# Softmax scaling of the larger half moved to ScalarE, and five weight units of the attention's queries multiplied as plain fp32

## The chip, the cores and the metric

The kernel runs on one core of one Trainium2 chip. The metric is the device time of one execution in microseconds (us). TensorE multiplies (PE in the profile, with PEld for its weight loads), VectorE is DVE, ScalarE is ACT, GpSimd is POOL, and SyncE (SP) issues the loads of the weights.

## The reference, cut to what matters

The reference is a stack of blocks on 256 tokens of width 1024 in fp32: feed-forward blocks, a recurrent block, one dilated attention, and two hybrid mixer layers. The change lies in the dilated attention alone:

```python
q = (x @ w_q).reshape(bsz, s, N_GROUPS, N_HEADS, HEAD_DIM)     # 3 groups, 16 heads of 64
scores = einsum("bpnqhd,bpnkhd->bpnhqk", qb, kw) / sqrt(dh)
scores = where(valid, scores - slope * distance, NEG_INF)
p = exp(scores - max(scores)); denom = sum(p)
out = einsum("bpnhqk,bpnkhd->bpnqhd", p / denom, vw)            # per group
out = sum over groups of softmax(log-sum-exp) * out             # then @ w_o
```

With one shared maximum per query, the sum over the three groups and the division by one common denominator give the same result as the softmax over the groups.

## The kernel before

All weights stream through one list of 537 units. A unit is 128 x 1024 fp32 (512 KB): eight 128 x 128 weight tiles in the order in which they are multiplied. SP loads each unit into one of five raw buffers (`RAWS = 5`, line 96). Then the unit is split for three fast multiplications: ACT rounds it to fp32r in two casts of 128 x 512 (`whi`, line 108), and DVE subtracts to get the remainder, again in two instructions of 128 x 512 (`wlo`, line 122). The raw buffer is free after the second subtraction. `whi` and `wlo` have seven buffers each, and `pump` prepares units up to `LOOK = 6` ahead of the one in use. The activations are held in two parts as well (`gh`, `gl`), so one weight tile costs three multiplications in `mm3` (line 174 through `mm`).

Units in the set `NATIVE` take another way: no cast and no subtraction, and one plain fp32 multiplication of the raw tile with the unsplit activations (`xf`, or `uc` and `xg`). Their raw buffer is free only when the last multiplication of the unit has read it. Before the change these are units 74 and 77 to 90 (the recurrent block: its gates and its GELU branch) and 347 to 352.

```python
def _hi(self):                          # lines 99 to 109
    ...
    if u in NATIVE:
        return
    ...
def mm3(self, out, w, xh, xl, start, stop, x=None):   # lines 176 to 182
    if w[1] is None:
        self.mm(out, w[0], x, start, stop)
        return
    self.mm(out, w[0], xh, start, False)
    self.mm(out, w[0], xl, False, False)
    self.mm(out, w[1], xh, False, stop)
```

The attention (`attn`, line 687) uses units 249 to 280. Units 249 to 252 are the first four query tiles, multiplied while the layer norm before is finished (`filler`). Units 253 and 254 hold the two tiles of the third group for head pairs 0 and 1, with the k index outside; 254 is k = 4 to 7. After that every two units make one call of `group`: for A = 2, 4, 6 units (A, groups 0 and 1), (A and A+1, group 2), (A+1, groups 0 and 1), so that 257 is (A=2, group 2), 260 the second tile of pair 3, 263 (A=4, group 2), and 266 the second tile of pair 5. Units 267 to 272 are pairs 6 and 7, and 273 to 280 the output projection.

Between the groups, `step` works a pipeline over heads (order in `PLAN`): `scores(h)` (12 multiplications on PE, bias and minimum on DVE line 744, exponential on ACT line 747), `soft(h-1)`, `trans(h-2)` (three transposes on PE, line 185, and a copy on ACT, line 768) and `pv(h-3)` (four multiplications). `put` (lines 724 and 725) splits the queries on ACT and DVE. POOL loads keys and values of the pairs (`K`, `W`, lines 700 and 701) and does the first addition of `soft`.

Dependences and the order on each engine come from the tile framework: it orders the instructions of each engine ahead of the run, by priority and by its own estimate of times, and inserts the waits. Each engine then runs its list in that order, so an instruction that waits holds up all behind it on its engine.

Of the kernel before, what the change touches and what calls it, by code (L numbers as in the profile page):

```python
# [12 lines left out]
AF = mybir.ActivationFunctionType  # L13
ALU = mybir.AluOpType
# [24 lines left out]
HOOKS = (1, 3, 5)  # L39
KVB = 5  # L40
RAWS = 5
NATIVE = {*range(347, 353), 74, 77, 78, 81, 84, 79, 80, 82, 83, *range(85, 91)}
RAW_LN = (LN_EMB - 1,)
LATE = {347: (6, 5)}

# [31 lines left out]
class Builder:  # L77
# [21 lines left out]
    def _hi(self):  # L99
# [3 lines left out]
        self.nhi += 1  # L103
        if u in NATIVE:
            return
# [5 lines left out]
    def _lo(self, pool=False):  # L111
# [3 lines left out]
        self.nlo += 1  # L115
        if u in NATIVE:
            return
# [16 lines left out]
    def w(self, spec, n=1):  # L134
# [3 lines left out]
        if o == 0:  # L138
            self.his.pop(u - 1, None)
            self.los.pop(u - 1, None)  # L140
            if u - 1 in NATIVE:
                self.raws.pop(u - 1)
# [7 lines left out]
        else:  # L150
            self.plan.extend(spec)
        if u in NATIVE:
            return self.raws[u][:, o * 128:(o + n) * 128], None
# [533 lines left out]
    def attn(self, ln_in, ln_out, eps):  # L687
        nc = self.nc
        N, off = SEQ, META
        with self.tc.tile_pool(name="attn", bufs=1) as p:  # L690
# [59 lines left out]
            def soft(h):  # L750
                s, den = S.pop(h), DEN.pop(h)
                nc.vector.reciprocal(den, den)
                t = p.tile([128, 384], F32, tag="t", name="t", bufs=4)
                for i, (a, n) in enumerate(((0, 256), (768, 128))):
                    o = t[:, 0:256] if i == 0 else t[:, 256:384]
                    nc.gpsimd.tensor_tensor(o, s[:, a:a + n], s[:, a + n:a + 2 * n], op=ALU.add)
                    nc.vector.tensor_tensor(o, o, s[:, a + 2 * n:a + 3 * n], op=ALU.add)  # L757
                    nc.vector.tensor_scalar(o, o, den[:, i:i + 1], None, op0=ALU.mult)
                S[h] = t

            def trans(h):
# [25 lines left out]
            def step(n=1):  # L787

                for _ in range(n):
                    i = next(steps)  # L790
                    if i < N_HEADS:
                        scores(i)
                    if 0 <= i - 1 < N_HEADS:
                        soft(i - 1)
                    if 0 <= i - 2 < N_HEADS:
                        trans(i - 2)
                    if 0 <= i - 3 < N_HEADS:
                        pv(i - 3)
# [714 lines left out]
```

## Time and profile before

| | |
|---|---|
| median of 3 runs | 1732.87 us (1731.61 to 1736.07) |
| profiled execution | 1732.95 us, span 1731.2 us |
| mean granted TensorE clock | 0.991 |
| PE busy | 1684.8 us (97%) |
| DVE busy | 1212.1 us (70%) |
| ACT busy | 1011.6 us (58%) |
| POOL busy | 166.0 us (10%) |

The span runs from the first to the last instruction of the profiled execution; 1.75 us of its time lie around it. Shares are averages over the whole span; the attention is some 7% of it. The granted clock is given as a share of 2.4 GHz: 1.00 is 2.4 GHz, 0.50 is 1.2 GHz. A plain fp32 multiplication of 128 x 256 leaves two records of TensorE in the trace, an fp32r one leaves one. Matmul records overlap, so the time that one takes is read from a stretch (busy time over count), not from its own duration.

### The profile page before, as it was taken

The page shows a single profiled execution, that of the slowest core. Times are in us where ns is not written, and L with a number is a line of the kernel's source. Part 1 is how long each engine was busy: PE and PEld are TensorE (multiplying, and loading weights), DVE is VectorE, ACT ScalarE, POOL GpSimd, SP SyncE. Part 2 cuts the span into 40 slices and gives each one's busy share as a digit, 9 for nine tenths or more (in the row PEclk, how much of TensorE's full clock was granted, in tenths as well). Part 3 has the DMA queues.
Part 4 walks back from the last instruction along what each step waited for, and adds up shares of the span by engine and source line. Part 5 has one row for each costly group of instructions (what it writes and reads, how often), then busy time and mean ns, then how long its engine had stood idle before and what let it go on. Part 6 is the DMA issues. An engine that isn't in the chain of part 4 may idle for free.

```text
span 1731.2 us, 34185 instructions
## 1 busy us (share of the span) xinstructions
PE 1684.8 (97%) x13420; PEld 1644.2 (95%) x13420; DVE 1212.1 (70%) x2377; ACT 1011.6 (58%) x2061; POOL 166.0 (10%) x240
## 2 busy tenths in 40 slices
PE   8999999999999999988999999899999999999996
PEld 8999999999999999988899999789999998999996
DVE  7666788965675666698897655878955577696653
ACT  6544756744575545576675455766744467585443
POOL 0001100000110000332110002121000122010011
PEclk9999999999999999989999999999999999999998
DMA  8555436555548655574236555243555545346550
GB/s 299 189 186 184 135 131 226 194 192 185 182 150 300 205 184 184 183 218 149 90 122 229 188 187 191 98 139 106 183 178 176 176 168 164 99 144 218 187 184 25
DMA packets 85594, 300.05 MB, mean 173 GB/s; under 512 B 11372, under 2 KB 13688, under 8 KB 85176
## 3 DMA queue, kind: packets, MB, share of 16 engines
q1 hardware_dynamic: 80216, 283.79, 49.2%
q0 software_dynamic: 2736, 9.61, 2.0%
q10 hardware_dynamic: 2480, 4.46, 0.8%
q8 instruction: 105, 1.72, 0.4%
q14 instruction: 57, 0.47, 0.1%
HBM read 292.47 MB, written 5.24 MB: 172 GB/s over the span
## 4 chain that ended last, share of the span: by engine, by line
PE 86%; DVE 7%; ACT 4%; issue 2%; DMA 1%; POOL 0%; DVEq 0%; SPq 0%; ACTq 0%
PE ps L174 86%; DVE wlo L122 2%; ACT whi L108 1%; PE ps L185 1%; DMA raw<-in_wst_dram 1%; DVE gl L258 1%; DVE q L725 1%; DVE s L744 1%; DVE xf L296 0%; DVE acc L235 0%; ACT q L724 0%; DVE xf L355 0%; DVE xf L354 0%; ACT fv L364 0%; DVE t L757 0%
## 5 line engine op out<-in xcount | busy, mean ns | idle before, releaser
L122 DVE TENSOR_TENSOR wlo<-raw,whi 128x512 fp32r<-128x512 f32 x1032 | 681.6, 697 | 332.6 <-ACT whi L108 331.5
L108 ACT CAST whi<-raw 128x512 fp32r<-128x512 f32 x1032 | 592.0, 617 | 493.4 <-issue 307.1
L174 PE MATMUL ps<-gh,whi 128*128 128x256 f32 (+3 forms) x2736 | 782.4, 287 | 7.4 <-ACT whi L108 6.7
L174 PE MATMUL ps<-gl,whi 128*128 128x256 f32 (+3 forms) x2736 | 777.6, 284 | 0.9 <-DVE gl L344 0.8
L174 PE MATMUL ps<-gh,wlo 128*128 128x256 f32 (+3 forms) x2736 | 774.4, 283 | 0.0
L174 PEld LDWEIGHTS ps<-gh,whi 128*128 128x128 f32 x2736 | 517.3, 189 | 11.5 <-ACT whi L108 7.9
L174 PEld LDWEIGHTS ps<-gl,whi 128*128 128x128 f32 x2736 | 518.8, 190 | 3.4 <-DVE gl L344 1.5
L174 PEld LDWEIGHTS ps<-gh,wlo 128*128 128x128 f32 x2736 | 519.4, 190 | 0.3 <-issue 0.2
L174 PE MATMUL ps<-hh,wlo 128*128 128x256 f32 (+1 forms) x1056 | 298.0, 282 | 0.0
L174 PE MATMUL ps<-hh,whi 128*128 128x256 f32 (+1 forms) x1056 | 297.9, 282 | 0.0
L174 PE MATMUL ps<-hl,whi 128*128 128x256 f32 (+1 forms) x1056 | 297.7, 282 | 0.0
L174 PEld LDWEIGHTS ps<-hl,whi 128*128 128x128 f32 x1056 | 199.0, 188 | 0.0
L174 PEld LDWEIGHTS ps<-hh,whi 128*128 128x128 f32 x1056 | 199.0, 188 | 0.0
L174 PEld LDWEIGHTS ps<-hh,wlo 128*128 128x128 f32 x1056 | 198.8, 188 | 0.0
L234 POOL TENSOR_TENSOR acc<-xf 128x256 f32<-128x256 f32 (+1 forms) x10 | 7.6, 756 | 1087.2 <-DVE xf L296 1085.0
L494 DVE TENSOR_TENSOR th<-th,ps 128x512 f32<-128x512 f32 (+1 forms) x62 | 42.9, 692 | 52.3 <-PE ps L174 52.2
L234 POOL TENSOR_TENSOR acc<-acc,xf 128x256 f32<-128x256 f32 (+1 forms) x50 | 46.9, 939 | 204.0 <-DVE xf L296 189.8
L296 DVE SCALAR_TENSOR_TENSOR xf<-ps,xf 128x256 f32<-128x256 f32 (+1 forms) x80 | 32.9, 423 | 43.0 <-PE ps L174 42.9
L239 ACT ACTIVATE sq<-xf 128x256 f32<-128x256 f32 (+1 forms) x88 | 35.6, 410 | 41.2 <-DVE xf L296 32.4
L252 ACT ACTIVATE gh<-xf,prm 128x256 fp32r<-128x256 f32 (+1 forms) x64 | 32.2, 509 | 46.4 <-DVE xf L296 46.4
L258 DVE SCALAR_TENSOR_TENSOR gl<-xf,prm,gh 128x256 fp32r<-128x256 f32 (+1 forms) x64 | 40.4, 638 | 11.0 <-ACT gh L252 11.0
L338 ACT ACTIVATE xf<-nt,prm 128x256 f32<-128x256 f32 (+1 forms) x72 | 42.6, 604 | 6.8 <-DVE nt L336 6.6
(319 smaller groups left out, 1842.0 us busy)
## 6 DMA issues: line engine op xcount, KB each, us to landing
raw<-in_wst_dram SPq DMA_DIRECT2D x537, 512.0 KB, 3.6
K<-khl POOLq DMA_DIRECT2D x32, 128.0 KB, 6.2
cst<-in_c_mix_dram POOLq DMA_DIRECT2D x2, 1202.0 KB, 5.8
khl<-kh ACTq DMA_DIRECT2D x4, 512.0 KB, 6.8
vsc<-kt ACTq DMA_DIRECT2D x4, 512.0 KB, 6.8
W<-vsc POOLq DMA_DIRECT2D x8, 256.0 KB, 5.8
out_dram<-xf SPq DMA_DIRECT2D x8, 128.0 KB, 1.7
dt<-in_c_dist_dram POOLq DMA_DIRECT2D x1, 576.0 KB, 9.6
```

The lines of the kernel that those rows point to most:

```text
L108: self.nc.scalar.copy(hi[:, q:q + 512], self.raws[u][:, q:q + 512])
L122: eng.tensor_tensor(lo[:, q:q + 512], r[:, q:q + 512], h[:, q:q + 512], op=ALU.subtract)
L174: self.nc.tensor.matmul(out, lhsT, rhs, start=start, stop=stop, skip_group_check=True)
L185: self.nc.tensor.matmul(out, in_, self.ident[0:n, 0:n], start=True, stop=True, is_transpose=True, skip_group_check=True)
L234: eng.tensor_tensor(a[:, 0, 0:N], x0, x, op=ALU.add)
L239: self.nc.scalar.activation(sq[:, 0:N], self.xf[:, m, off:off + N], AF.Square)
L252: return self.nc.scalar.activation((self.xg if ln in RAW_LN else self.gh)[:, m, c], self.xf[:, m, off:off + N], AF.Copy, scale=g)
L258: return self.nc.vector.scalar_tensor_tensor(self.gl[:, m, c], self.xf[:, m, off:off + N], g, self.gh[:, m, c].bitcast(F32), op0=ALU.mult, ...
L296: self.nc.vector.scalar_tensor_tensor(x, banks[m][:, 0:N], coef, x, op0=ALU.mult, op1=ALU.add)
L338: nc.scalar.activation(self.xf[:, i, off:off + N], t, AF.Identity, scale=g, bias=b)
L494: nc.vector.tensor_tensor(th, th, pu, op=ALU.mult)
L725: nc.vector.scalar_tensor_tensor(Q[pr][e][b, g], src[a], sc, hi.bitcast(F32), op0=ALU.mult, op1=ALU.subtract)
```

## The change

Two edits. Units 254, 257, 260, 263 and 266 join `NATIVE`: for each, two casts on ACT and two subtractions on DVE are left out, 24 fp32r multiplications become 8 plain fp32 ones on `xf`, and the raw buffer is held until PE has used it. In `soft(h)`, the multiplication with the reciprocal denominator of the 128 x 256 half (queries 128 to 255) goes from DVE (line 758) to ACT; that of the 128 x 128 half stays on DVE.

```diff
-NATIVE = {*range(347, 353), 74, 77, 78, 81, 84, 79, 80, 82, 83, *range(85, 91)}
+NATIVE = {254, 257, 260, 263, 266, *range(347, 353), 74, 77, 78, 81, 84, 79, 80, 82, 83, *range(85, 91)}
...
                     nc.gpsimd.tensor_tensor(o, s[:, a:a + n], s[:, a + n:a + 2 * n], op=ALU.add)
                     nc.vector.tensor_tensor(o, o, s[:, a + 2 * n:a + 3 * n], op=ALU.add)
-                    nc.vector.tensor_scalar(o, o, den[:, i:i + 1], None, op0=ALU.mult)
+                    if i == 0:
+                        nc.scalar.activation(o, o, AF.Copy, scale=den[:, i:i + 1])
+                    else:
+                        nc.vector.tensor_scalar(o, o, den[:, i:i + 1], None, op0=ALU.mult)
```

## Rows read from the trace of the kernel before

**Rows 1.** The page: busy time by engine, and the chain's shares.
```profile
PE 1684.8 (97%) x13420; PEld 1644.2 (95%) x13420; DVE 1212.1 (70%) x2377; ACT 1011.6 (58%) x2061; POOL 166.0 (10%) x240
...
PE 86%; DVE 7%; ACT 4%; issue 2%; DMA 1%; POOL 0%; DVEq 0%; SPq 0%; ACTq 0%
```

**Rows 2.** Stretches: length, busy us per engine (instructions), clock, DMA share, GB/s.
```profile
core 0: us, PE busy (x) PEld busy (x) DVE busy (x) ACT busy (x) POOL busy (x), PEclk, DMA share, GB/s
741.50:865.00 123.50, 110.44 (x828) 105.83 (x828) 105.03 (x249) 83.01 (x182) 35.01 (x61) 0.93 0.49 145
886.70:1076.00 189.30, 189.30 (x1584) 188.24 (x1585) 123.09 (x212) 107.15 (x207) 11.91 (x16) 1.00 0.56 185
236.00:265.00 29.00, 29.00 (x137) 25.51 (x136) 20.84 (x36) 20.08 (x35) 0.00 (x0) 1.00 0.44 145
770.00:790.00 20.00, 16.94 (x127) 16.36 (x126) 19.00 (x47) 13.66 (x31) 6.71 (x11) 0.91 0.48 144
790.00:810.00 20.00, 19.10 (x154) 18.37 (x153) 17.94 (x43) 13.55 (x30) 6.64 (x12) 1.00 0.54 173
```

**Rows 3.** Halved clock: the three stretches of it in the attention.
```profile
758.42:768.66 10.24, 7.71 (x34) 7.45 (x35) 7.55 (x18) 5.12 (x12) 4.12 (x8) 0.50 0.52 154
782.30:785.72 3.42, 3.42 (x16) 3.15 (x15) 3.42 (x12) 2.61 (x7) 1.06 (x2) 0.50 0.45 153
816.44:819.86 3.42, 3.10 (x13) 2.92 (x14) 2.35 (x10) 2.71 (x7) 1.09 (x2) 0.50 0.47 153
```

**Rows 4.** PE's timeline: start, us, instruction, [idle before it, who ended it].
```profile
762.18 1.09 PE L174 MATMUL ps<-K,q 128*128 128x256 f32 x4 [2.50 <-DVE m L744]
...
781.58 0.88 PE L185 MATMUL ps<-ident,t 128*128 128x128 f32 x6 [3.06 <-DVE q L725]
...
814.84 1.00 PE L174 MATMUL ps<-K,q 128*128 128x128 f32 x7 [1.30 <-DVE q L725]
...
816.76 0.90 PE L185 MATMUL ps<-ident,t 128*128 128x128 f32 x3 [0.76 <-DVE m L744]
```

**Rows 5.** The chain in order of time, 752 to 782: start, us, what.
```profile
752.10 7.81 DMA raw<-in_wst_dram
759.93 0.62 ACT whi L108
760.55 0.38 ACT q L724
...
773.09 0.96 DVE t L758 x2
774.05 1.48 DVE wlo L122 x2
...
779.85 0.55 DVE t L758 x2
```

**Rows 6.** Line 108 from the start to 759.90 us: count, ns min/median/max.
```profile
L108 ACT CAST whi<-raw x496: 601/618/666, 6.0 to 754.8; 128x512 fp32r<-128x512 f32 x166
```

**Rows 7.** Line 174, plain fp32 in the recurrent block: count, ns min/median/max.
```profile
L174 PE MATMUL ps<-xf,raw x160: 379/379/379, 236.5 to 277.7; 128*128 128x256 f32 x160
```

**Rows 8.** Groups by form, 741.5 to 865: count, busy us, mean ns, idle before.
```profile
L122 DVE TENSOR_TENSOR wlo<-raw,whi 128x512 fp32r<-128x512 f32 x47 | 31.7, 696 | 1.7 <-ACT whi L108 1.3
L108 ACT CAST whi<-raw 128x512 fp32r<-128x512 f32 x46 | 27.5, 615 | 21.1 <-PE ps L174 17.6 <-DMA raw<-in_wst_dram 3.3
...
L758 DVE TENSOR_SCALAR t<-t,den 128x256 f32<-128x256 f32 x16 | 6.1, 384 | 0.0
```

**Rows 9.** Line 291, a scaled copy on ACT: count, ns min/median/max.
```profile
L291 ACT ACTIVATE xf<-xf,prm x16: 492/509/512, 1028.6 to 1717.8; 128x256 f32<-128x256 f32 x16
```

**Rows 10.** Waits, 741 to 865: total us, times, longest us.
```profile
DVE t L757 <- POOL t L756: 9.0, 8, 1.5
```

**Rows 11.** Waits of SP's queue, 741 to 865: total us, times, longest us.
```profile
SPq L96 <- DVE wlo L122: 101.1, 22, 9.4
```

**Rows 12.** The page: loads of the weights, KB, median us to landing.
```profile
raw<-in_wst_dram SPq DMA_DIRECT2D x537, 512.0 KB, 3.6
```

## Prediction

> **What bounds the kernel now.** I read the page first: PE is busy 97% of the span and carries 86% of the chain [rows 1]. That average hides the place of the change, so next I cut the span into stretches [rows 2]. The block after the attention is PE alone: 189.30 us of work in 189.30 us, so whatever the attention gives back there is kept to the end. The attention from 741.5 to 865 us is different: PE is busy 110.44 of 123.50 us, at a mean clock of 0.93, while DVE is busy 105.03 and ACT 83.01 us. PE therefore loses 13.06 us by idling. It also loses by the clock: three stretches run at 0.50, which is 1.2 GHz, and PE is busy 7.71, 3.42 and 3.10 us in them [rows 3]; half of the 14.23 us, 7.1 us, is lost there. 13.1 + 7.1 = 20.2 us is all that the attention could ever give.
>
> PE's timeline shows whom it waited for around these stretches [rows 4], and the chain why [rows 5].
>
> Place 1, 758 to 769 us: PE idles 2.50 us. The chain goes back over a query split on ACT (760.55) to a cast (759.93) that waited for a weight load issued at 752.10, 7.81 us before. 496 casts precede that one [rows 6], two for each of 248 split units; with the 15 native units among the first 263, it is unit 263. ACT stood still behind this cast, with the query split that PE needed queued after it. The clock is at 0.50 from 758.42 to 768.66.
>
> Place 2, 778 to 786 us: PE idles 3.06 us for a query split on DVE. DVE is busy 19.00 of 20.00 us from 770 to 790 [rows 2]: it is the bound there. The 0.50 stretch begins at 782.30, right after that idle time.
>
> Place 3, 813 to 820 us: PE idles 1.30 and 0.76 us, again for DVE, with a 0.50 stretch of 3.42 us over and after it.
>
> **The change, part by part.** Sums are made against the profiled execution, 1732.95 us (span 1731.2 and 1.75 around it); the median of the runs is 1732.87, so nothing is to be carried over.
>
> PE's own work. The recurrent block runs plain fp32 units only between 236 and 265 us: 29.00 us busy for 137 records, 211.7 ns each [rows 2]. Line 174 has 160 such records for 10 units of 8 tiles [rows 7], so a tile has two: 423 ns. Three fp32r multiplications are 3 x 189.30 / 1584 = 3 x 119.5 = 358.5 ns [rows 2]. The change costs 65 ns a tile, and 5 x 8 x 0.065 = 2.6 us in all. That is the term against it. The Trainium skill (FP8 and Floating Point Precision, "TensorE Precision Notes") counts true fp32 as four passes through the array; taken as four times 119.5 ns, an estimate from that page, a tile would cost 478 ns, the term would be 4.8 us and the sum below 1727.7. The row's 423 ns is the same operation in the same shape, so it decides.
>
> DVE. Ten subtractions at 0.696 us and sixteen scalings at 0.384 us go [rows 8]: 7.0 + 6.1 = 13.1 us less, of which, going by the order of the units, those of 260, 263 and 266 (4.2 us) and all scalings fall inside the crowded stretch from 755 us on.
>
> ACT. Ten casts at 0.615 us go: -6.2 us [rows 8]. Sixteen scalings of 128 x 256 come: no row has them on ACT, but line 291 is the same operation (scaled copy, fp32, 128 x 256, a pointer as scale) at 0.509 us [rows 9], so +8.1 us. As bounds I take DVE's 0.384 for the same work and a cast's 0.615 us (twice the columns, no scale): 6.1 to 9.8 us. Net +2.0 us, bounds 0 and +3.6, on an engine that is idle 40.5 of the stretch's 123.5 us [rows 2]; what of it can lie on the chain stands under the rest, below.
>
> Place 1. Unit 263 is native now: the cast that waited does not exist. The 2.50 us come back. Of the clock's loss, 7.71 / 2 = 3.9 us, I take half, since DVE and ACT are crowded just before 758 too, when the clock falls: 1.9 us. Together 4.4; bounds 0 (another cast waits for its load in the same place) and 6.4.
>
> Place 2. Before DVE reaches the query split that PE waits for, it now skips the large scalings of heads 0 to 2 (3 x 0.384) and the subtractions of 263 (1.48 us at 774.05, [rows 5]): 2.6 of the 3.06 us. With 0.4 us of idling left I take the 1.7 us of clock as regained: 4.3; bounds 0 and 4.8.
>
> Place 3. DVE has skipped another five scalings and 266's subtractions (1.9 + 1.4 us) by then, but PE was busy 19.10 of 20.00 us from 790 to 810 [rows 2] and cannot come much sooner. Of 2.06 + 1.55 us I take half, 1.8; bounds 0 and 3.6.
>
> The rest, 820 to 865 us: nine heads scaled on ACT instead of DVE, 0.125 us longer each, and no unit of the change is left. About half of 1.1 us can lie on the chain: +0.5; bounds -1 and +1.1.
>
> Waits that are added. (a) ACT's scaling waits for DVE's addition, which waits for POOL's; DVE waited 9.0 us for POOL in 8 cases, 1.5 at most [rows 10]. Behind it on ACT are casts, exponentials and the copies of transposed probabilities, for all of which PE waits. I cost it at nothing, because exponentials of the next head can stand before it on ACT and cover the additions; without that cover it is rival C. (b) The raw buffers of five units are freed by PE and not by DVE, and all later loads queue on SP behind. SP already waits 101.1 us for subtractions here, 22 times [rows 11], so it is far ahead; and from 236 to 265 us, with native units only and the same five buffers, PE never idles: 29.00 of 29.00 us [rows 2]. I cost it at nothing. If that cover fails, one late load is 3.6 us [rows 12], or 7.81 while keys and values load [rows 5]. No DMA is added or moved to another queue; POOL's work is unchanged.
>
> Sum: 2.6 - 4.4 - 4.3 - 1.8 + 0.5 = -7.4 us: 1725.5 us.
>
> **Rivals.**
>
> A, the forecast: the three waits shrink as costed. With three quarters of what I took for places 1 to 3 (-7.9 for -10.5) it is 1728.2, with their upper bounds (-14.8) 1721.3: 1721 to 1728.
>
> B, no change to be measured: the wait of place 1 moves to another unit. Held buffers make the loads around 262 to 264 start as late as 752 us again, in the stretch where keys and values load, and the next cast waits in 263's stead. Then place 1 gives nothing: -3.0, 1729.9; with place 2 halved as well 1732. For it: loads took 7.81 us there. Against: unit 264 was cast only at 769, so ACT has other work to do first. So 1728 to 1736.
>
> C, slower: ACT becomes the pacing engine. In place of 0.384 us on DVE each head costs ACT 0.509 plus POOL's wait, 9.0 / 16 = 0.56 us, with everything queued behind: 16 x 1.07 = 17.1, less 6.2 of casts is 10.9 us. It decides when the scaling stands in ACT's order before the casts that PE needs next. If half of what places 1 to 3 return comes all the same, +10.9 + 2.6 - 5.3 gives 1741.2; 1736 to 1746 (nothing of it comes). For it: one late cast was enough to stop ACT in place 1. Against: ACT is idle a third of the stretch. The Trainium skill (TensorE: Matmul & The Clock Gate, "Architectural detail") calls ACT's and DVE's queues strictly first in, first out; the trace agrees at place 1, where the casts' wait for a load, 3.3 us [rows 8], kept the query split back.
>
> D, more: all three places close. 20.2 - 2.6 = 17.6 is the limit, 1715.3; so 1715 to 1721.
>
> **How the numbers follow.** A has 0.52, B 0.25, C 0.16, D 0.07. About 0.3%, 5.2 us, is what a measurement of this kernel can tell from no change, so faster means under 1727.7 and slower over 1738.1. A lies below 1727.7 in 0.48, D wholly; C lies above 1738.1 in 0.14; the rest of A and C and all of B lie between: faster 0.55, same 0.31, slower 0.14. A alone is 1721 to 1728. The range that leaves out two in ten drops most of C and the depth of D: 1718 to 1738.
>
> **What would show it.** Right: no cast waits for its load around 756 to 760 us, the query splits follow one another there, and the 0.50 stretches of [rows 3] shrink in number or length; the 741.5 to 865 us stretch ends some 7 us sooner, with DVE some 10 us less busy; scalings on ACT near 0.51 us; plain fp32 tiles near 423 ns at full clock. Wrong: a new wait of a cast for its load (B); ACT idle before the scaling with casts right behind, and PE waiting for them (C). What I can least see beforehand is the new order in which the framework sets each engine's list: it decides which instruction stands behind a wait, and so which of A, B and C comes.

## The result and the profile after

The changed kernel takes 1746.55 us in the median of 4 runs (1743.66 to 1749.12), beside 1734.09 us (1731.61 to 1736.07, 4 runs) for the kernel before: a ratio of 1.0069 [1.0054, 1.0083]. It is 12.5 us slower, where 7.4 us less was forecast. The profiled execution took 1749.12 us, its span is 1747.3 us. Every ratio in this document is an estimate from the executions of both kernels, with its 95% interval in brackets; it can differ by 0.1% from the ratio of the medians beside it, and one slow execution (3777.47 us, of the kernel with the scaling behind the exponentials) is left out of it.

The page of the changed kernel, its busy times, its chain and the loads of the weights, against [rows 1] and [rows 12]:

```profile
PE 1690.3 (97%) x13380; PEld 1646.5 (94%) x13380; DVE 1199.1 (69%) x2351; ACT 1015.5 (58%) x2067; POOL 174.3 (10%) x240
...
PE 84%; DVE 7%; ACT 4%; issue 2%; DMA 1%; POOL 1%; ACTq 0%; SPq 0%; DVEq 0%; POOLq 0%
...
raw<-in_wst_dram SPq DMA_DIRECT2D x537, 512.0 KB, 4.1
```

All that the change was to remove is removed: DVE is busy 13.0 us less (1212.1 to 1199.1, forecast 13.1). PE is busy 5.5 us more, forecast 2.6; most of the rest is clock, as the next view shows. The same stretch of the attention as in [rows 2], and its stretches at half clock, which stand beside [rows 3]; columns as there:

```profile
741.50:865.00 123.50, 104.76 (x708) 97.42 (x706) 87.14 (x202) 79.15 (x172) 34.17 (x57) 0.92 0.43 138
...
748.95:755.76 6.81, 6.63 (x19) 5.30 (x20) 6.67 (x18) 6.66 (x19) 3.09 (x6) 0.50 0.65 193
772.83:776.24 3.41, 3.41 (x17) 3.41 (x18) 2.70 (x6) 1.59 (x3) 0.00 (x0) 0.50 0.74 237
786.48:793.31 6.83, 5.39 (x20) 4.86 (x21) 5.31 (x13) 4.42 (x11) 1.77 (x4) 0.50 0.48 155
827.44:830.85 3.41, 3.41 (x11) 2.76 (x10) 2.27 (x10) 2.76 (x9) 1.62 (x3) 0.50 0.39 142
```

Every engine is busy less in these 123.5 us, PE by 5.7 us: DVE has less to do, and part of everyone's work now lies behind 865 us. PE's idle time rose from 13.06 to 18.74 us, and its work at 1.2 GHz from 14.23 to 18.84 us.

Where the time goes is read best from PE's transposes (line 185), three for each head: their start against the kernel before. The work of PE between them is not quite the same. From head 0 to head 5 the trace has 42 weight tiles before the change and 48 after it (32 split, 16 plain): six tiles of the queries, some 2.2 us at 3 x 119.5 ns, that stood ahead of head 0 now stand behind it. At heads 3, 5, 10 and 15 PE has the same multiplications behind it in both kernels.

```
head        0      1      3      4      5     10     15
before    771.1  781.6  788.1  792.7  803.4  839.1  864.4
after     772.8  787.9  796.5  802.7  813.5  849.6  876.3
later      +1.7   +6.3   +8.4  +10.0  +10.1  +10.5  +11.9
```

By head 5, 10 us are lost, and they are never given back: the block of PE alone [rows 2] begins 11.9 us later. Three views show what stands behind the first heads. ACT's timeline, in the layer norm ahead of the attention (start, us, instruction, [idle before it, who ended it]), and the count of casts up to 748.2 us:

```profile
740.01 0.60 ACT L338 ACTIVATE xf<-nt,prm 128x256 f32<-128x256 f32 x1
748.13 0.62 ACT L108 CAST whi<-raw 128x512 fp32r<-128x512 f32 x1 [7.52 <-DMA raw<-in_wst_dram]
748.65 0.40 ACT L341 CAST gh<-xf 128x256 fp32r<-128x256 f32 x1
...
L108 ACT CAST whi<-raw x487: 604/620/663, 6.5 to 748.1; 128x512 fp32r<-128x512 f32 x163
```

486 casts, those of 243 split units, precede this one. Of units 0 to 260, 18 are native now, so it is unit 261. Its load landed at 747.77 us, no later than before (748.18); before, the cast was wanted only at 752.90. Right behind it stands the rounding of a normed tile (line 341) that PE needs. PE's timeline:

```profile
749.11 0.58 PE L174 MATMUL ps<-gh,whi 128*128 128x256 f32 x1 [5.44 <-ACT gh L341]
...
752.81 5.08 PE L174 MATMUL ps<-xf,raw 128*128 128x256 f32 x16
...
766.15 3.62 PE L174 MATMUL ps<-xf,raw 128*128 128x256 f32 x16
769.42 0.82 PE L174 MATMUL ps<-K,q 128*128 128x256 f32 x4
...
787.92 0.90 PE L185 MATMUL ps<-ident,t 128*128 128x128 f32 x3 [4.60 <-DVE q L725]
```

PE idles 5.44 us at 749, where it did not wait before, and is then granted 1.2 GHz from 748.95 to 755.76 us. The idling and the half clock (6.63 / 2 = 3.3 us) make 8.8 us, and PE is only 1.7 us late at head 0, 3.9 at equal work: some 5 us did come back, as place 1 was to give. Then it idles 4.60 us before head 1 (before: 3.06). The chain shows what stands ahead of it:

```profile
737.06 10.71 DMA raw<-in_wst_dram
...
768.01 4.82 DMA raw<-in_wst_dram
...
772.86 0.63 ACT whi L108
...
778.44 0.76 POOL t L756
...
779.23 0.66 DVE t L757
779.89 0.09 DVE den L752
...
780.00 0.51 ACT t L759
780.51 0.52 ACT whi L108
...
781.05 0.69 DVE wlo L122
...
783.01 0.50 DVE q L725
```

A load issued only at 768.01 (unit 264, issued at 754.98 before) holds a cast; then the new scaling on ACT (780.00) waits for POOL and DVE, with a cast behind it, with DVE's subtraction and query split behind that. Both edits are in this one chain. The waits of ACT from 741 to 877 us, and of SP's queue from 733 to 877 us (total us, times, longest):

```profile
ACT whi L108 <- DMA raw<-in_wst_dram: 10.0, 3, 7.5
ACT t L759 <- DVE den L752: 7.5, 9, 1.3
ACT t L759 <- DVE t L757: 2.0, 2, 1.4
...
SPq L96 <- DVE wlo L122: 97.5, 18, 18.7
SPq L96 <- PE ps L174: 13.7, 4, 6.2
```

Against [rows 8] the casts' wait for loads has tripled (3.3 to 10.0 us), and 9.5 us of waiting before the scaling are new.

### The profile page after: what moved, and what is told of

Read it like the earlier page. It is cut to its first block, busy times and chain, and to the rows that moved or that the text cites. A ratio compares the mean times of both kernels' runs of the same rounds, so it can differ in the third digit from the quotient of the medians.

```text
span 1747.3 us, 34071 instructions
## 1 busy us (share of the span) xinstructions
PE 1690.3 (97%) x13380; PEld 1646.5 (94%) x13380; DVE 1199.1 (69%) x2351; ACT 1015.5 (58%) x2067; POOL 174.3 (10%) x240
## 4 chain that ended last, share of the span: by engine, by line
PE 84%; DVE 7%; ACT 4%; issue 2%; DMA 1%; POOL 1%; ACTq 0%; SPq 0%; DVEq 0%; POOLq 0%
PE ps L174 84%; DVE wlo L122 2%; DMA raw<-in_wst_dram 1%; ACT whi L108 1%; DVE q L725 1%; ACT s L747 1%; PE ps L185 1%; DVE gl L258 1%; DVE s L744 1%; DVE xf L296 0%; ACT q L724 0%; POOL t L756 0%; DVE t L757 0%; DVE acc L235 0%; POOL acc L234 0%
## 5 line engine op out<-in xcount | busy, mean ns | idle before, releaser
L174 PE MATMUL ps<-gh,whi 128*128 128x256 f32 (+3 forms) x2696 | 770.9, 286 | 12.8 <-ACT whi L108 7.2
L174 PE MATMUL ps<-gl,whi 128*128 128x256 f32 (+3 forms) x2696 | 765.9, 284 | 0.5 <-DVE gl L344 0.4
L174 PE MATMUL ps<-gh,wlo 128*128 128x256 f32 (+3 forms) x2696 | 763.0, 283 | 0.0
L174 PEld LDWEIGHTS ps<-gh,whi 128*128 128x128 f32 x2696 | 509.2, 189 | 17.1 <-ACT whi L108 8.2
L174 PEld LDWEIGHTS ps<-gl,whi 128*128 128x128 f32 x2696 | 510.6, 189 | 3.1 <-DVE gl L344 1.4
L174 PEld LDWEIGHTS ps<-gh,wlo 128*128 128x128 f32 x2696 | 511.3, 190 | 0.5 <-issue 0.5
L234 POOL TENSOR_TENSOR acc<-xf 128x256 f32<-128x256 f32 (+1 forms) x10 | 13.0, 1300 | 1088.1 <-DVE xf L296 935.6
L174 PE MATMUL ps<-xf,raw 128*128 128x256 f32 x240 | 57.0, 397 | 0.9 <-DVE ol L190 0.9
L174 PEld LDWEIGHTS ps<-xf,raw 128*128 128x128 f32 x240 | 47.9, 202 | 8.1 <-DVE ol L190 1.1
```

The costliest lines, as they stand in the source:

```text
L174: self.nc.tensor.matmul(out, lhsT, rhs, start=start, stop=stop, skip_group_check=True)
L234: eng.tensor_tensor(a[:, 0, 0:N], x0, x, op=ALU.add)
```

## The experiments

The theory: two separate losses. (1) With the casts of 257 and 260 gone, the cast of 261 moved up in ACT's list to before its load lands. (2) The scaling on ACT waits for DVE's sums with casts behind it. Rivals: only one of the edits costs anything; the loads are late because keys and values load first; the raw buffers held by PE are the cause; DVE was no bound, so that nothing was to be had. The kernel before was run beside the experiments: median 1732.85 us (14 runs) for e1 to e4, 1732.15 (25) for e5 to e8, 1733.36 (25) for e9 to e12. Each kernel gets new lists from the framework, so an edit can also shift instructions that it does not name. In the expectations (1) is called the late-load theory, (2) the ACT-pacing theory, and the raw buffers held by PE the held-buffer theory.

**e1: the five native units alone** (the first edit of the diff, scaling left on DVE).

> The five native units without the move of the scaling. Late-load theory (the casts that are left out bring ACT's list to the cast of unit 261 in the middle of the layer norm, before its load has landed): the whole loss is here, 1743 to 1749 us, ACT waiting some 7 us for unit 261's load near 741 to 748 us. ACT-pacing theory (rival C: the scaling stops ACT): the loss is gone, 1728 to 1734 us. Held-buffer theory (PE frees five raw buffers late): 1740 to 1747 us, but the wait is at later loads (262 to 265), not at 261.

1740.03 us, ratio 1.0051 [1.0033, 1.0069]. ACT's waits, 741 to 877 us:

```profile
ACT whi L108 <- DMA raw<-in_wst_dram: 10.0, 4, 6.2
```

The stop in the layer norm is there without the scaling, 6.2 us of ACT at 261's cast and 4.1 us of PE (7.52 and 5.44 with both edits): it belongs to the native units. The time lies under the 1743 to 1749 us of the late-load theory and at the lower end of the held-buffer theory's range; the longest wait is at 261, as the first has it, and 2.67 us are at 264, as the second has it.

**e2: the scaling alone** (the second edit of the diff, units as before).

> The move of the scaling without the native units. Late-load theory: within 4 us of the kernel before (1730 to 1737 us), with the old wait at unit 263's cast still there. ACT-pacing theory: 1740 to 1747 us. Held-buffer theory: as the late-load theory.

1737.78 us, 1.0035 [1.0022, 1.0048]. ACT's waits, 741 to 877 us:

```profile
ACT t L759 <- DVE den L752: 5.5, 7, 1.3
ACT t L759 <- DVE t L757: 4.2, 3, 1.8
ACT whi L108 <- DMA raw<-in_wst_dram: 2.9, 1, 2.9
```

9.7 us of waiting for DVE's sums, while the casts wait for a load as little as before. The two parts add up: 0.51% + 0.35% = 0.86% beside the 0.69% measured for both, within the intervals. Both edits are slower each by itself.

**e3: the changed kernel with the cast of unit 261 kept behind the layer norm.** The edit asks for nothing but this place in ACT's list; the framework's new lists also differ in a few other places of the attention, on ACT and on DVE.

```diff
+        with ExitStack() as after:
+            if u == 261:
+                after.enter_context(self.tc.issue_after(self.normed.ins))
             for q in range(0, UNIT * 128, 512):
                 self.nc.scalar.copy(hi[:, q:q + 512], self.raws[u][:, q:q + 512])
...
-                nc.scalar.copy(self.gh[:, k, 0:N], self.xf[:, k, off:off + N])
+                self.normed = nc.scalar.copy(self.gh[:, k, 0:N], self.xf[:, k, off:off + N])
```

> The changed kernel with one thing different: the two casts of unit 261 may not stand in ACT's list before the layer norm's last cast. Late-load theory: PE's 5.4 us of idling at 744 to 749 us go, and most of the halved clock after it (3.3 us): 1736 to 1741 us; what then remains over the kernel before is the plain multiplications (2.6 us) and the later waits at 264 and 265. ACT-pacing theory: no change, 1745 to 1749 us. Held-buffer theory: at most 3 us faster, 1743 to 1747 us.

1735.83 us, 1.0021 [1.0011, 1.0032]. ACT's wait for loads from 741 to 877 us (lines are three further on), and the half-clock stretches that are left:

```profile
ACT whi L111 <- DMA raw<-in_wst_dram: 4.1, 3, 1.7
...
781.32:784.73 3.41, 3.41 (x15) 3.23 (x16) 3.38 (x10) 1.84 (x4) 0.00 (x0) 0.50 0.46 154
818.86:822.28 3.42, 3.16 (x11) 2.38 (x10) 2.59 (x10) 2.42 (x6) 0.69 (x2) 0.50 0.45 153
```

The place of one unit's cast in ACT's list was worth 0.48% of the 0.69%: part (1) of the theory is shown. PE's 5.44 us of waiting in the norm are gone, and head 0 starts at 766.4 us for 772.8, with the same tiles behind both: 6.4 us of the 7.7 that head 15 gains (868.6 for 876.3). Two of the four stretches at 1.2 GHz went with it. Head 15 is still 4.2 us later than in the kernel before.

**e4: two pairs fewer of keys and values ahead** (changed kernel, `KVB = 5` to `KVB = 3`), to see whether they make 261's load late.

> The changed kernel with three pairs of keys and values loaded ahead instead of five: the same order on ACT (unit 261's cast in the middle of the layer norm), but two fifths fewer loads beside unit 261's. Late-load theory: unit 261 lands sooner, ACT's wait of 7.5 us shrinks to 2 to 5, 1739 to 1744 us, unless pairs come late later on. ACT-pacing and held-buffer theories: no faster than 1745 us.

1744.80 us, 1.0069 [1.0048, 1.0089]; the wait for loads is 10.6 us, 7.9 the longest. No effect, and little could be expected: the two pairs left out are issued from 745.58 us on in the changed kernel, 2.2 us before 261's load lands. Which transfers hold that load up for 10 us this did not show, since three pairs and the distance table still load beside it.

**e5 and e9: a sixth raw buffer, in the changed kernel and in the kernel before.** It takes the place of a buffer of `wlo`, so the second run is needed to read the first.

```diff
-RAWS = 5
+RAWS = 6
...
-        lo = self.p_w.tile([128, UNIT * 128], F32R, tag="wlo", name="wlo")
+        lo = self.p_w.tile([128, UNIT * 128], F32R, tag="wlo", name="wlo", bufs=NBUF - 1)
```

> The changed kernel with six raw buffers instead of five, paid for with six wlo buffers instead of seven. It leaves unit 261's cast inside the layer norm, but its loads and those of 262 to 265 need not wait for the buffers that the native units hold. Held-buffer theory: the second loss (about 4.5 us between the transposes of heads 0 and 1) goes, and unit 261's load starts earlier too: 1736 to 1742 us. Late-load theory alone (only the place of the cast counts): 1744 to 1749 us.

> Control for e5: the kernel before, with six raw buffers and six wlo buffers. If the six wlo buffers are what made e5 slow outside the attention, this kernel shows the same loss there (some 10 us against the kernel before, 1740 to 1745 us) and its attention ends where that of the kernel before does (last transposes near 864 us). If the native units need the wlo buffers, it is within 4 us of the kernel before.

The changed kernel: 1748.27 us, 1.0103 [1.0084, 1.0123]; the kernel before: 1745.60 us, 1.0070 [1.0054, 1.0085]. The time of the changed kernel alone would fit the late-load theory, but the exchange of a `wlo` buffer for a raw one costs the kernel before 0.7% as well, all but 0.9 us of it outside the attention. Between the two, the change costs only 1.0103 / 1.0070 = 1.0033 (some 0.0025 either way by the two intervals) instead of 1.0069, and in the attention head 15 starts at 867.9 against 865.3 us: 2.6 us later in place of 11.9. From head 0 to head 5 the changed kernel takes 35.9 us with the sixth buffer, at full clock, and 40.7 without it for the same multiplications. More raw buffers remove most of the loss in the attention. That fits held buffers; since a sixth buffer also lets 262's load start sooner (741.96 us for 756.20) and shortens the stop in the norm (PE's wait 4.1 us for 5.44), it doesn't prove them the only cause.

**e6: native units with the cast of 261 behind the norm, scaling on DVE** (the first edit of the diff and the edit of e3).

> The five native units with unit 261's cast kept behind the layer norm, and the scaling left on DVE. If the losses are separate and add up (cast 261 some 9 us, scaling some 6 us): 1728 to 1733 us, no slower than the kernel before. If the scaling's loss appears only together with the native units or only by chance of the order: 1734 to 1739 us.

1734.21 us, 1.0017 [1.0008, 1.0027]; were the losses separate, 1728 to 1733 us was expected. Head 0 starts at 764.7 us, 6.4 before the kernel before, of which 2.2 are the six tiles that now stand behind it: 4.2 at equal work. Up to 763 us PE waits at most 0.24 us at a time, and ahead of head 0 it is nowhere at half clock. At head 5 (805.1), where the work is equal, it is 1.7 us behind: 5.9 us are lost between. The stretch, beside 771.0 to 803.4 us before (220 records of PE in both, but 48 weight tiles here and 42 there):

```profile
764.70:805.10 40.40, 34.93 (x220) 32.52 (x220) 30.53 (x73) 22.60 (x49) 11.54 (x20) 0.87 0.52 169
```

It takes 40.4 us where it took 32.4 (PE 28.58 busy, clock 0.95 there). PE idles 5.5 instead of 3.8 us. Of the 6.35 us that it is busy longer, some 2.2 are the six tiles more, 1.0 the 16 plain ones (65 ns each), and the rest, some 3 us, the clock: three stretches of 3.42 us at 1.2 GHz for one. Units 262 and 264 are loaded only when the subtractions of 259 (748.16) and 261 (761.37) end, at 748.24 and 761.43 us (before 745.07 and 754.98): native units hold three of the five raw buffers, 257, 260 and 263 the second time.

**e7: the scaling on ACT behind the exponentials of a later head** (scaling alone, moved into `trans(h)`), so that it never waits for sums; `self.exped` is the last exponential issued.

```diff
...
             def trans(h):
-                t = S.pop(h)
+                t, den = S.pop(h), DEN.pop(h)
+                with self.tc.issue_after(self.exped.ins):
+                    nc.scalar.activation(t[:, 0:256], t[:, 0:256], AF.Copy, scale=den[:, 0:1])
...
```

> Scaling on ACT without native units, but each scaling may stand in ACT's list only behind the exponentials of the head two later, so that its sums are long done. If what costs in the move is ACT's waiting for DVE's sums (9.7 us in all): 1730 to 1734 us, and ACT waits under 2 us for its scalings. If it is ACT's added work of 8 us and the later start of the transposes: 1736 to 1740 us.

1734.68 us, 1.0015 [1.0006, 1.0025], in place of 1.0035; the median lies between the two ranges that were expected. PE's wait for it, 741 to 877 us:

```profile
PE ps L185 <- ACT t L765: 4.9, 7, 1.2
```

By the middle of the intervals, which just overlap, over half of the scaling's loss went with ACT's wait; now PE's transposes wait for the scaling, and it is still no gain.

**e8: the larger half not scaled at all** (line 758 for that half left out, on units as before). It asks what DVE's 6.1 us of scaling [rows 8] are worth at most.

> The kernel before without the scaling of the larger half (queries 128 to 255 of each head are not divided by their sum), no native units: DVE has 6.1 us less to do and ACT nothing more. The prediction took DVE as the bound at its places 2 and 3: then 1727 to 1730 us. If DVE's list is not what sets the stage's end (its waits for ACT and the loads do): 1731 to 1735 us.

1733.14 us, 1.0008 [0.9998, 1.0017]. The two stretches of [rows 2] and PE's wait at place 2:

```profile
770.00:790.00 20.00, 17.12 (x128) 16.50 (x127) 19.02 (x45) 13.53 (x31) 6.81 (x11) 0.91 0.51 153
741.50:865.00 123.50, 109.25 (x835) 104.71 (x834) 102.44 (x234) 83.91 (x184) 35.22 (x60) 0.96 0.49 146
...
780.88 0.55 PE L185 MATMUL ps<-ident,t 128*128 128x128 f32 x3 [2.80 <-DVE q L725]
```

In the kernel before, DVE waits for ACT ahead of place 2:

```profile
770.26 0.75 DVE L725 SCALAR_TENSOR_TENSOR q<-ps,qs,q 64x512 fp32r<-64x512 f32 x1 [1.00 <-ACT q L724]
```

Nothing that the runs could tell. DVE is just as full from 770 to 790 us (19.02 for 19.00), since other work moves up. The query split that PE waits for at place 2 starts at 780.34 us for 781.03, 0.7 us sooner, and PE waits 2.80 us for it where it waited 3.06. DVE has no idle time between its wait for ACT (1.00 us before, 1.09 here) and that split; of the three scalings ahead of the split the first stands ahead of this wait. At head 5 the gain is gone (804.5 for 803.4 us). The full row shows where DVE works, and not what work taken from it is worth. The framework also orders DVE's list otherwise here from 764 us on, so the run tells what the edit is worth, and not the missing work by itself.

**e10, e11, e12: fewer native units: 254 and 257; 260, 263 and 266; 263 alone** (scaling on DVE, ACT's order left to the framework).

> Only 254 and 257 native, scaling on DVE. They are the two whose casts stood before and in the layer norm. Late-load theory: the cast of unit 260 now stands in the middle of the layer norm in ACT's list; its load is issued some 4 us before that of 261, so ACT waits 2 to 5 us there: 1734 to 1740 us. Held-buffer theory alone: two held buffers are both free by 766 us, no loss: 1730 to 1734 us.

> Only 260, 263 and 266 native, scaling on DVE. ACT's list through the layer norm is that of the kernel before. Late-load theory: no stop in the layer norm and no cast of 263 any more: 1726 to 1733 us. Held-buffer theory: three buffers are held together from 755 us on, the loads of 264 to 266 start late, and the gain of place 1 is given back: 1731 to 1736 us.

> Only unit 263 native, scaling on DVE: the one cast that the prediction wanted gone. If its wait goes as the prediction costed it (4.4 us, less 0.5 us for the plain multiplications): 1727 to 1730 us. If the next cast, of unit 264, waits in its place: within 2 us of the kernel before, and ACT's wait for a load near 757 to 762 us is still there, at 264.

1736.16 us, 1.0021 [1.0012, 1.0031]; 1733.66 us, 1.0000 [0.9991, 1.0010]; 1732.24 us, 0.9998 [0.9989, 1.0008]. ACT's and PE's timelines with 254 and 257 native:

```profile
743.14 0.62 ACT L108 CAST whi<-raw 128x512 fp32r<-128x512 f32 x1 [2.30 <-DMA raw<-in_wst_dram]
...
758.52 1.14 ACT L108 CAST whi<-raw 128x512 fp32r<-128x512 f32 x2 [3.60 <-DMA raw<-in_wst_dram]
...
760.73 1.97 PE L174 MATMUL ps<-K,q 128*128 128x256 f32 x8 [3.27 <-DVE q L725]
```

and ACT's with 263 alone:

```profile
760.18 0.62 ACT L108 CAST whi<-raw 128x512 fp32r<-128x512 f32 x1 [2.31 <-DMA raw<-in_wst_dram]
```

In each, the cast next in line waits instead: 260 in the norm and 262 at place 1; 264 at 761.80 (2.06 us) with three native; 264 at 760.18 with one. With 263 alone the next cast waits 2.31 us, beside 3.3 us of all casts in [rows 8]. Head 0 starts 3.0 us sooner than before (768.1), head 1 2.8 (778.8), head 15 only 1.6 (862.8), too little for the runs to tell. As in rival B, the wait moves on to the next unit. None of the three is measurably faster than the kernel before.

## Why the prediction was wrong

**Place 1, the step that failed first.** "The cast that waited does not exist" was right, and its return came: with the cast of 261 held back, head 0 is 4.2 us sooner at equal work, beside the 4.4 taken. What failed is that the edits on ACT were costed as time removed from it, and not as a new order: with 261 up to some 12 us sooner in ACT's list (wanted at 740.6 us, cast at 752.90 before) and its load issued when it was before (737.06 for 736.83), a wait of 7.52 us arose in the layer norm. Rival B had the mechanism, the wait moving to another unit's cast, but put it at place 1 and took it for no loss. Its size is shown by the runs with that cast held back: 0.48% with the scaling on ACT, 0.34% (5.9 us) without. The prediction cited the Trainium skill (TensorE: Matmul & The Clock Gate, "Architectural detail") for the strict order of ACT's queue; the trace agrees, with 7.52 us of ACT and 5.44 us of PE behind one cast. The queue's order was known, and what would stand in it was not worked out.

**Wait (b), costed at nothing, was wrong.** The cover named, the recurrent block, has native units only; in the attention they alternate with split ones, and three held buffers of five leave two for the units whose casts ACT needs. SP now waits 13.7 us for PE, unit 264's load starts 13 us later, and two casts wait 0.73 and 1.80 us just before head 1. The native units with 261's cast held back, with no stop in the norm and no scaling on ACT, still lose 5.9 us from head 0 to head 5, more than place 1 returned; the two runs with a sixth buffer point the same way. The prediction read SP's 101.1 us of waiting for subtractions [rows 11] as a lead, and the trace says the reverse: 264's load was issued at 754.98 us before, right behind 259's last subtraction (754.92), so SP stood waiting for a free buffer, and a buffer held longer delays the load. How much of the 5.9 us is the held buffers and how much ACT's order was not separated.

**Wait (a), costed at nothing, was wrong; rival C's mechanism came.** It priced the wait at 9.0 us; it measured 9.5 us with both edits and 9.7 with the scaling alone. The exponentials of the next head, which were to cover it, do not stand before it: at 780.00 us it follows those of its own head (777.34 and 778.27). Its price on the end was smaller than C's 10.9: 6.1 us, of which the order behind the exponentials recovers 3.5 (1.0035 to 1.0015, intervals that just overlap).

**Places 2 and 3: what is taken from DVE did not pass to PE.** "It is the bound there" holds as far as DVE has no idle time before the split of place 2. What failed is the size: 2.6 us of the 3.06 were to go. Leaving out the scalings, 1.2 us of the 2.6, brought the split 0.7 us sooner, and nothing of it reached the end. 263's subtractions, the other 1.5 us, did not shorten place 2 either: with 263 alone native, head 1 gains nothing beyond the 3.0 us of head 0, and DVE waits 0.85 us for POOL ahead of it (771.46 us). The 4.3 and 1.8 us of the sum rested on DVE's saving reaching PE and then the end.

**What was right.** PE's own work: unit 257 begins at 766.15 us and the next multiplication at 769.42, 3.27 us for 8 tiles at full clock or 409 ns a tile, beside the 423 ns taken. The 478 ns that the prediction worked out from the four passes of the Trainium skill (FP8 and Floating Point Precision, "TensorE Precision Notes") are further off: the row was the better guide. ACT's scaling takes 0.51 us as read from [rows 9], ten subtractions and casts are gone, and the half-clock stretches follow waits of PE as in [rows 3] and [rows 4].

The sum in place of -7.4 us, each part from its own run: the native units +8.8 us (1.0051 of 1732.9), of which 5.9 us are 261's cast and 2.9 us (1.0017) stay with that cast held back, about PE's 2.6, with place 1's return lost again between heads 0 and 5; the scaling +6.1 us (1.0035). The parts make 14.9 us alone and 12.5 together, which the intervals allow.

## What to carry to other kernels

When instructions are taken out of an engine's list, write down what moves up into their place and when its input lands: a load that was early enough for the old order can be late for the new one. A row that shows an engine 95% busy does not tell what a piece of work taken from it is worth; leave the work out in a trial before counting its removal as a gain. A buffer that a later engine frees can delay later loads of its ring, also those of units that the change does not touch. And when two kernels are compared at a mark in the middle, count whether the same work lies behind it.

## What was not expected of the hardware

GpSimd's first addition of a later layer norm (line 234, 128 x 272 fp32) took eight times as long in the profiled execution of the changed kernel as before; the timeline of GpSimd there, and then that of the kernel before:

```profile
1094.30 6.25 POOL L234 TENSOR_TENSOR acc<-xf 128x272 f32<-128x272 f32 x1 [2.19 <-DVE xf L355]
```

```profile
1082.41 0.78 POOL L234 TENSOR_TENSOR acc<-xf 128x272 f32<-128x272 f32 x1 [2.18 <-DVE xf L355]
```

The chain has 5.65 us of it as "issue" at 1094.84. PE is 14.2 us late behind it (1106.05 for 1091.86), after 11.9 us before it, so 2.3 of the 16.1 us between the two profiled spans come with it, and not from the attention. None of the experiments' profiles has it, and its cause is open. And the 512 KB load of unit 261 took 10.71 us, where the median load takes 4.1. In the kernel before it took 11.4 (736.83 to 748.18); keys, values and the distance table load beside it in both, and what holds it up is open.
